# The end of a down projection: one row pair more left over, another tile order, and sums in an order written out by hand

## The chip, the cores and the metric

The kernel runs on one core of a Trainium2 chip. Its metric is the device time of one execution in microseconds (us). The engines are named as the profile names them: PE is TensorE (matrix products), DVE is VectorE, ACT is ScalarE, POOL is GpSimd, SP is SyncE, which here only issues transfers (DMAs).

## The reference

One decoder layer on 512 tokens of width 1024, in float32: a conditioned mixer (mLSTM heads beside a convolution group), then a causal ConvFFN. The change touches only the last product of the ConvFFN and the normalised, gated addition that follows it:

```python
u = rms_norm(x, ffn_pre_g[l]) * (1.0 + sc2) + sh2
up = causal_dwconv(u @ ffn_up[l], ffn_conv_w[l], ffn_conv_b[l])
a, gt = jnp.split(up, 2, axis=-1)
f = (jax.nn.silu(gt) * a) @ ffn_down[l]          # 512 x 2816 by 2816 x 1024
x = x + g2 * rms_norm(f, ffn_post_g[l])
```

`rms_norm` needs the sum of squares over a token's whole row of 1024 before any of its outputs can be scaled.

## The kernel before

**The down projection in seven products.** `f` is 512 tokens by 1024 columns and is computed as a two by two block product with seven products in place of eight. The contraction over 2816 rows runs in `NM` = 11 row pairs (`m`, two blocks of 128 rows each). Each of the products p1 to p7 has two accumulators in PSUM, one for each `q` (128 tokens of a half of 256). Every float32 operand is split in two parts, `h` and `l`, and `mm3` makes one product of 128x128 by 128x512 out of three matmuls.

A first phase runs p1, p5, p6 and p7 over all pairs and leaves sums of them in SBUF: `sp1`, `su`, `s3`, `sp5`. A second phase runs p2, p3 and p4 (`prod2`). The output has four tiles of 128 tokens, `tt` 0 to 3, each in two halves (`hf`) of 512 columns; `q = tt % 2`. Tiles 0 and 1 are p2 + sp1 and p3 + su. Tiles 2 and 3 are p4 + s3 in their first half; their second half is `sp5`, complete since the first phase, squared and already multiplied by the gain row (L1104).

**The second phase's loop (L1106 to L1122).** For each pair `m` the operands are made: `forms_g2(m)` (the activation side, L1034) and `forms2(m)` (the weight side, L1025: one subtraction, then `parts` splits `b2`, `b4` and `t4` into `h` on ACT and `l` on VectorE). Then SP issues transfers: for four of the values of `m` a pair of loads of the residual rows (`xrs`, L1110 to L1114, tied to `M2`), then `load2(m + 3)` (three loads of weight parts, L1019) and `load_g2(m + 5)`. For `m < M2` all eighteen matmuls of the pair follow: p2, p3 and p4, each for both `q`. The pairs from `M2` on are left for the end.

**The end (L1123 to L1142).** For each tile in turn the left pairs' matmuls are run, and then, for each half that is not complete, a sum (PSUM plus SBUF, L1134), a sum of squares on ACT (`sq_sum`, L608: an ACTIVATE and a read of its accumulator) and a scaling by the gain row (L1137). `token_factor` (L612) then makes the tile's factor: a 128x1 step on VectorE (L615) and a power on POOL (L617). Two output steps follow (L1141), each with a store, the first half's from SP's queue and the second half's from ACT's.

**What sets the order.** The instructions of PE and SP stay in the order of the program. VectorE, ACT and POOL are ordered by a planner at build time, which takes, of what its own model of time holds ready, the instruction that stands earliest in the program. `in_order()` is a block in which those three engines too keep the order that is written, by ordering edges that are no instructions; until now it is used elsewhere, not in the second phase. Weight parts rotate through 20 buffers (`wpool`), six for each pair; raw weights through two `raws` and the two halves of `more`.

Of the kernel before, what the change touches and what calls it, by code (L numbers as in the profile page):

```python
# [14 lines left out]
ALU = mybir.AluOpType  # L15
# [4 lines left out]
T = 512  # L20
KT = D // P
NT = T // P
# [30 lines left out]
def decoder_layer(ctx, tc, w_glu0, x, c, adaT, vecs, w_glu, w_qko, w_v0, w_v, w_out, w_up, w_down, out):  # L53
    nc = tc.nc
    V, S, G, PE = nc.vector, nc.scalar, nc.gpsimd, nc.tensor
# [13 lines left out]
    @contextmanager  # L69
    def in_order():  # L70

        traced = nc.cur_bb.bb.instructions
        first = traced[-1]
        yield
        a = next(i for i in reversed(range(len(traced))) if traced[i] is first) + 1
        last = {}
        for ins in traced[a:]:
            if ins.engine in (V.engine, S.engine, G.engine):
                if ins.engine in last:
                    tc.add_manual_dep(ins, last[ins.engine].name, mybir.DependencyInfo(mybir.DependencyClass.NoSync, mybir.DependencyReason.DATA),  # L80
                                      reason="program order")
                last[ins.engine] = ins

    def slot(name, dt=F32):
        return slots.tile([P, T], dt, tag="t", name=name)
# [100 lines left out]
    def mm3(ps, a, b, start, stop):  # L186

        PE.matmul(ps, a[0], b[0], start=start, stop=False)  # L188
        PE.matmul(ps, a[0], b[1], start=False, stop=False)  # L189
        PE.matmul(ps, a[1], b[0], start=False, stop=stop)  # L190
# [28 lines left out]
    first = []  # L219
# [25 lines left out]
    for tt in range(NT):  # L245
# [11 lines left out]
        if tt == NT - 1:  # L257
# [9 lines left out]
                    op0=ALU.add)  # L267
    g32 = const.tile([P, KT], F32, name="g32")
    V.tensor_scalar(out=g32, in0=vcols("mix_pre_g", 0, KT), scalar1=RD, scalar2=None, op0=ALU.mult)
    xr = [slot(f"xr{j}") for j in range(KT)]  # L270
# [32 lines left out]
    for k in range(KT):  # L303
        wk = []
        r = adas.tile([P, D], F32, tag="ada", name=f"wglu0_{k}")
# [285 lines left out]
    def row(i, make, name, queue=nc.scalar):  # L591

        rows = make(name) if make is not cvtile else [make(f"{name}r{hf}") for hf in range(2)]
        for hf, r in enumerate(rows):
            queue.dma_start(r, rows_d[i][hf * T : (hf + 1) * T].partition_broadcast(P))
        return rows
# [8 lines left out]
    def cvtile(name):  # L605
        return cvs.tile([P, T], F32, tag="cvs", name=name)

    def sq_sum(src, col, name):  # L608
        junk = small.tile([P, T], BF16, tag="junk", bufs=1, name=f"{name}junk")
        S.activation(junk, src, AF.Square, accum_out=col)  # L610

    def token_factor(sq, name):  # L612

        t = small.tile([P, 1], F32, tag="tt", name=f"{name}t")
        V.tensor_scalar(out=t, in0=sq[:, :1], scalar1=sq[:, 1:2], scalar2=D * EPS, op0=ALU.add, op1=ALU.add)  # L615
        r = small.tile([P, 1], F32, tag="tr", name=f"{name}r")
        G.tensor_tensor(out=r, in0=t, in1=mhalf[:, :1], op=ALU.pow)  # L617
        return r

    def tok(tt):  # L620
        return slice(tt * P, (tt + 1) * P)
# [171 lines left out]
    def chain_sums(tt):  # L793

        ps = banks[tt]
        sq_sum(ps, msq[:, 2 * tt + 1 : 2 * tt + 2], f"mixb{tt}")
        un = adas.tile([P, D], F32, tag="ada", name=f"un{tt}")
        uns[tt] = [un[:, :T], un[:, T:]]
        V.tensor_tensor(out=uns[tt][1], in0=ps, in1=g1r[1], op=ALU.mult)
        return token_factor(msq[:, 2 * tt : 2 * tt + 2], f"rm{tt}")  # L800

    def chain_x(tt, r):

        xsq = small.tile([P, 2], F32, tag="xsq", name=f"xsq{tt}")
        for hf, m in enumerate((mg[tt], uns[tt][1])):
            V.scalar_tensor_tensor(out=x1[tt][hf], in0=m, scalar=r, in1=x1[tt][hf], op0=ALU.mult, op1=ALU.add)
            sq_sum(x1[tt][hf], xsq[:, hf : hf + 1], f"x1_{tt}_{hf}")
        for hf, un in enumerate(uns[tt]):
            V.tensor_tensor(out=un, in0=x1[tt][hf], in1=gs2r[hf], op=ALU.mult)
        return token_factor(xsq, f"rf{tt}")  # L810
# [53 lines left out]
    with in_order():  # L864
# [3 lines left out]
        r = chain_sums(0)  # L868
        up_split(1, raw1, slots, "t")
        r = chain_x(0, r)  # L870
# [3 lines left out]
        r = chain_sums(1)  # L874
        up_split(1, raw1, slots, "t")
        r = chain_x(1, r)
# [4 lines left out]
        r = chain_sums(2)  # L881
        turn_out(1)
        r = chain_x(2, r)
# [4 lines left out]
        r = chain_sums(3)  # L888
        up_split(2, raw2, wpool, "w")
        r = chain_x(3, r)  # L890
# [29 lines left out]
    NM = NF // 2  # L920
# [26 lines left out]
    for i in range(NF):  # L947
        if i < NE:
            pa, pg = early[i]
        else:  # L950
# [4 lines left out]
            if i == 19:  # L955
# [4 lines left out]
                g2r = row(3, lambda n: [wide[:, :T], wide[:, T:]], "g2")  # L960
# [15 lines left out]


    M1 = NM - 2
    M2 = NM - 2
    fsq = const.tile([P, 2 * NT], F32, name="fsq")  # L980
    p1 = [atbank(f"p1_{q}") for q in range(2)]
    p5 = [cvbank(f"p5_{q}") for q in range(2)]
# [42 lines left out]
    def forms2(m):  # L1025

        r = loaded.pop(m)
        V.tensor_tensor(out=quarter(r, 2), in0=quarter(r, 0), in1=quarter(r, 2), op=ALU.subtract)
        return parts(r, [(f"b2_{m}", 0), (f"b4_{m}", 1), (f"t4_{m}", 2)])

    def load_g2(m):
        nc.sync.dma_start(kept[:, m % 5, :], g2_d[m])
# [8 lines left out]
    def part(form, q):  # L1041
        return tuple(z[:, q * P : (q + 1) * P] for z in form)
# [53 lines left out]
    def prod2(m, which, q):  # L1096
        a12, a22, s4 = g2[m]
        ps, form, w = {"p2": (p2, a12, "b2"), "p3": (p3, s4, "b4"), "p4": (p4, a22, "t4")}[which]
        mm3(ps[q], part(form, q), w2[m][w], m == 0, m == NM - 1)
# [5 lines left out]
    xrs = []  # L1105
    for m in range(NM):  # L1106
        if m >= G2A:
            g2[m] = forms_g2(m)
        w2[m] = forms2(m)
        if M2 - NT <= m < M2:  # L1110
            tt = m - M2 + NT
            xrs.append([cvtile(f"xr{tt}_{hf}") if tt < 2 else slot(f"xr{tt}_{hf}") for hf in range(2)])
# [4 lines left out]
        if m + 5 < NM:  # L1117
            load_g2(m + 5)
        if m < M2:
            for which in ("p2", "p3", "p4"):  # L1120
                for q in range(2):
                    prod2(m, which, q)  # L1122
    for tt in range(NT):  # L1123
        q = tt % 2
        for which in ("p2", "p3") if tt < 2 else ("p4",):
            for m in range(M2, NM):
                prod2(m, which, q)
        res, xr = [], xrs[tt]
        for hf, pair in enumerate(((p2[q], sp1[q]), (p3[q], su[q])) if tt < 2 else ((p4[q], s3[q]), None)):
            if pair is None:  # L1130
                res.append(sp5[q])
                continue
            ps, z = pair
            V.tensor_tensor(out=z, in0=ps, in1=z, op=ALU.add)  # L1134
            sq_sum(z, fsq[:, 2 * tt + hf : 2 * tt + hf + 1], f"dn{tt}_{hf}")
            m = slot(f"fo{tt}_{hf}")
            V.tensor_tensor(out=m, in0=z, in1=g2r[hf], op=ALU.mult)  # L1137
            res.append(m)
        r = token_factor(fsq[:, 2 * tt : 2 * tt + 2], f"ro{tt}")
        for hf in range(2):  # L1140
            V.scalar_tensor_tensor(out=res[hf], in0=res[hf], scalar=r, in1=xr[hf], op0=ALU.mult, op1=ALU.add)  # L1141
            (nc.scalar if hf else nc.sync).dma_start(out[tok(tt), hf * T : (hf + 1) * T], res[hf])  # L1142


def _layout(i):
# [65 lines left out]
```

## Time and profile before

| what | value |
|---|---|
| median of 3 runs | 783.6 us (783.5 to 783.65) |
| profiled execution, its own time | 782.93 us |
| its span, first to last instruction | 781.2 us |
| mean granted TensorE clock | 0.996 |
| VectorE busy over the span | 590.7 us in 938 instructions |
| ACT busy | 407.6 us |
| POOL busy | 384.8 us |
| DMA moved | 124.28 MB, mean 159 GB/s |

In timelines a row has the start (us from the span's start), the duration, the engine, the line in the kernel, the operation, the tile written and the tiles read (buffer numbers left out, so `p` is any of p1 to p7 and `t_10l` is the `l` part of a weight form of pair 10), shapes, and in brackets the idle time before it with what ended it. Durations overlap at their ends: the next instruction of an engine starts before the one ahead of it has fully drained, so prices are read from start to start.

### The profile page before, as it was taken

Reading aid. Unit: us, or ns where it says so; the run is one execution under the profiler, and the core shown is the slowest. Engines: PE = TensorE matmul, PEld = TensorE weight load, DVE = VectorE, ACT = ScalarE, POOL = GpSimd, SP = SyncE. Lnnn points to the kernel's source line nnn. Section 1 sums busy time; section 2 is a strip of 40 time slices with the busy share of each in tenths; the row PEclk is TensorE's granted clock in tenths of the full one; section 3 lists DMA queues with packets and bytes.
Section 4 is the critical chain, followed back from the end, with each engine's and each line's share of the span. In section 5 each row is a group of like instructions: output and inputs, shape, how many; then the busy total and the mean of one; then the engine's idle time right before and its main releaser. Section 6 shows DMA issues by size and latency. Waiting matters only on the chain.

```text
span 781.2 us, 10573 instructions
## 1 busy us (share of the span) xinstructions
PE 762.0 (98%) x3683; PEld 635.5 (81%) x3683; DVE 590.7 (76%) x938; ACT 407.6 (52%) x766; POOL 384.8 (49%) x313
## 2 busy tenths in 40 slices
PE   7899999999999999999999999999999999999995
PEld 4688898878888888888888998888888888888883
DVE  6659999999999433555868798666555678698986
ACT  6576428668655554482244545444444444456752
POOL 3689758779779434333661456444445440000001
PEclk9999999999999999999999999999999999999998
DMA  8983213303117432424962653332233321778852
GB/s 291 327 300 122 105 60 108 135 29 109 55 60 248 152 110 79 147 108 151 380 220 83 259 205 136 128 128 98 99 121 122 128 99 51 285 258 263 296 205 107
DMA packets 35977, 124.28 MB, mean 159 GB/s; under 512 B 4146, under 2 KB 5586, under 8 KB 29908
## 3 DMA queue, kind: packets, MB, share of 16 engines
q1 hardware_dynamic: 24084, 95.15, 34.5%
q10 hardware_dynamic: 11840, 28.46, 10.2%
q8 instruction: 29, 0.48, 0.2%
q14 instruction: 24, 0.20, 0.1%
HBM read 112.17 MB, written 11.42 MB: 158 GB/s over the span
## 4 chain that ended last, share of the span: by engine, by line
PE 80%; DVE 14%; DMA 2%; ACT 1%; POOL 1%; issue 1%; SPq 0%; DVEq 0%; POOLq 0%; ACTq 0%
PE up L189 10%; PE up L188 10%; PE up L190 10%; DVE cv L661 6%; PE p L190 4%; PE p L188 4%; PE p L189 4%; PE glu L189 3%; PE glu L190 3%; PE glu L188 3%; PE qko L188 3%; PE qko L189 3%; PE qko L190 3%; PE mixa L190 2%; PE mixa L188 2%; PE mixa L189 2%
## 5 line engine op out<-in xcount | busy, mean ns | idle before, releaser
L661 DVE SCALAR_TENSOR_TENSOR cv<-gt,cvw,cv 128x506 f32<-128x506 f32 (+24 forms) x200 | 134.3, 730 | 0.4
L617 POOL TENSOR_TENSOR ro0r<-ro0t,mhalf 128x1 f32<-128x1 f32 x1 | 0.9, 925 | 125.8 <-DVE ro0t L615 125.8
L171 POOL TENSOR_TENSOR wup_1024l<-wup,wup_1024h 128x512 fp32r<-128x512 f32 x20 | 27.3, 1367 | 31.7 <-ACT wup_1024h L170 27.9
L171 POOL TENSOR_TENSOR wup_0l<-wup,wup_0h 128x512 fp32r<-128x512 f32 x20 | 27.7, 1387 | 29.8 <-ACT wup_0h L170 29.8
L657 POOL TENSOR_TENSOR cs<-cs,cs 128x510 f32<-128x510 f32 (+3 forms) x32 | 41.8, 1308 | 0.2
L171 POOL TENSOR_TENSOR wup_1536l<-wup,wup_1536h 128x512 fp32r<-128x512 f32 x20 | 28.2, 1409 | 27.4 <-ACT wup_1536h L170 27.4
L189 PE MATMUL up<-u2l,wup_0h 128*128 128x512 f32 (+1 forms) x100 | 36.5, 365 | 0.2 <-DVE u2l L830 0.2
L188 PE MATMUL up<-u2h,wup_0h 128*128 128x512 f32 (+1 forms) x100 | 36.5, 365 | 0.0
L188 PE MATMUL up<-u2h,wup_1024h 128*128 128x512 f32 (+1 forms) x100 | 36.4, 364 | 0.0
L190 PE MATMUL up<-u2h,wup_0l 128*128 128x512 f32 (+1 forms) x100 | 36.4, 364 | 0.0
L188 PE MATMUL up<-u2h,wup_512h 128*128 128x512 f32 (+1 forms) x100 | 36.4, 364 | 0.0
L189 PE MATMUL up<-u2l,wup_512h 128*128 128x512 f32 (+1 forms) x100 | 36.4, 364 | 0.0
L188 PE MATMUL up<-u2h,wup_1536h 128*128 128x512 f32 (+1 forms) x100 | 36.4, 364 | 0.0
L189 PE MATMUL up<-u2l,wup_1536h 128*128 128x512 f32 (+1 forms) x100 | 36.4, 364 | 0.0
L190 PE MATMUL up<-u2h,wup_512l 128*128 128x512 f32 (+1 forms) x100 | 36.4, 364 | 0.0
L190 PE MATMUL up<-u2h,wup_1536l 128*128 128x512 f32 (+1 forms) x100 | 36.4, 364 | 0.0
L190 PE MATMUL up<-u2h,wup_1024l 128*128 128x512 f32 (+1 forms) x100 | 36.4, 364 | 0.0
L189 PE MATMUL up<-u2l,wup_1024h 128*128 128x512 f32 (+1 forms) x100 | 36.3, 363 | 0.0
L155 DVE SCALAR_TENSOR_TENSOR junk<-ada,cb 128x1024 bf16<-128x1024 f32 x20 | 30.8, 1542 | 5.6 <-DMA ada<-in_adaT 5.3
L171 POOL TENSOR_TENSOR wup_512l<-wup,wup_512h 128x512 fp32r<-128x512 f32 x20 | 27.2, 1360 | 14.6 <-ACT wup_512h L170 14.6
L655 ACT ACTIVATE cs<-gt,cvw 128x511 f32<-128x511 f32 (+4 forms) x40 | 27.2, 713 | 5.0 <-POOL cs L657 4.1
L171 POOL TENSOR_TENSOR wqko_1024l<-wqko,wqko_1024h 128x512 fp32r<-128x512 f32 x12 | 16.6, 1382 | 21.8 <-PE v L189 12.3
(1061 smaller groups left out, 2682.1 us busy)
## 6 DMA issues: line engine op xcount, KB each, us to landing
wup<-in_w_up SPq DMA_DIRECT2D x22, 1024.0 KB, 7.3
wqko<-in_w_qko SPq DMA_DIRECT2D x12, 1024.0 KB, 4.9
ada<-in_adaT ACTq DMA_DIRECT2D x20, 512.0 KB, 5.5
ada<-in_adaT SPq DMA_DIRECT2D x16, 512.0 KB, 5.8
wo<-in_w_out SPq DMA_DIRECT2D x8, 1024.0 KB, 9.3
spare<-in_adaT ACTq DMA_DIRECT2D x12, 512.0 KB, 7.5
wglu<-in_w_glu SPq DMA_DIRECT2D x5, 1024.0 KB, 7.7
wd<-in_w_down SPq DMA_DIRECT2D x6, 768.0 KB
```

The source lines that it names most:

```text
L155: t = V.scalar_tensor_tensor(out=junk, in0=r, scalar=1.0, in1=cb, op0=ALU.mult, op1=ALU.mult, accum_out=mod[:, i : i + 1])
L171: (eng or G).tensor_tensor(out=lo[:, :n], in0=src, in1=hi[:, :n].bitcast(F32), op=ALU.subtract)
L188: PE.matmul(ps, a[0], b[0], start=start, stop=False)
L189: PE.matmul(ps, a[0], b[1], start=False, stop=False)
L190: PE.matmul(ps, a[1], b[0], start=False, stop=stop)
L617: G.tensor_tensor(out=r, in0=t, in1=mhalf[:, :1], op=ALU.pow)
L655: S.activation(t[:, d:], cvx[j][:, : T - d], AF.Copy, scale=w(CK - 1 - d))
L657: G.tensor_tensor(out=side[:, d:], in0=side[:, d:], in1=t[:, d:], op=ALU.add)
L661: last_tap = V.scalar_tensor_tensor(out=cp[:, d:], in0=cvx[j][:, : T - d], scalar=w(CK - 1 - d), in1=cp[:, d:], op0=ALU.mult, op1=ALU.add)
```

## The change

`M2` goes from `NM - 2` to `NM - 3`: pair 8 is no longer run in the loop, and three pairs are left for the end. The residual loads, tied to `M2`, move from `m` = 5 to 8 to `m` = 4 to 7. The end takes tiles 2 and 3 first, then 0 and 1. Sums, squares, scalings, factors, output steps and stores are cut into small functions and written in one fixed order, inside `in_order()`. Of tiles 2 and 3 the second half is stored first. No arithmetic is added or taken away.

```diff
-    M2 = NM - 2
+    M2 = NM - 3
...
-    for tt in range(NT):
-        q = tt % 2
+    def last_products(tt):
         for which in ("p2", "p3") if tt < 2 else ("p4",):
             for m in range(M2, NM):
-                prod2(m, which, q)
-        res, xr = [], xrs[tt]
+                prod2(m, which, tt % 2)
+
+    def last_sums(tt, only=None):
+
+        q, res = tt % 2, []
         for hf, pair in enumerate(((p2[q], sp1[q]), (p3[q], su[q])) if tt < 2 else ((p4[q], s3[q]), None)):
+            if only not in (None, hf):
+                continue
             if pair is None:
                 res.append(sp5[q])
                 continue
             ps, z = pair
             V.tensor_tensor(out=z, in0=ps, in1=z, op=ALU.add)
             sq_sum(z, fsq[:, 2 * tt + hf : 2 * tt + hf + 1], f"dn{tt}_{hf}")
+            res.append(z)
+        return res
+
+    def last_scale(tt, res, first=0):
+        for n in range(1 if tt >= 2 else len(res)):
+            hf = n + first
             m = slot(f"fo{tt}_{hf}")
-            V.tensor_tensor(out=m, in0=z, in1=g2r[hf], op=ALU.mult)
-            res.append(m)
-        r = token_factor(fsq[:, 2 * tt : 2 * tt + 2], f"ro{tt}")
-        for hf in range(2):
-            V.scalar_tensor_tensor(out=res[hf], in0=res[hf], scalar=r, in1=xr[hf], op0=ALU.mult, op1=ALU.add)
-            (nc.scalar if hf else nc.sync).dma_start(out[tok(tt), hf * T : (hf + 1) * T], res[hf])
+            V.tensor_tensor(out=m, in0=res[n], in1=g2r[hf], op=ALU.mult)
+            res[n] = m
+        return res
+
+    def last_factor(tt):
+        return token_factor(fsq[:, 2 * tt : 2 * tt + 2], f"ro{tt}")
+
+    def last_out(tt, res, r, hf):
+        V.scalar_tensor_tensor(out=res[hf], in0=res[hf], scalar=r, in1=xrs[tt][hf], op0=ALU.mult, op1=ALU.add)
+        (nc.scalar if hf else nc.sync).dma_start(out[tok(tt), hf * T : (hf + 1) * T], res[hf])
+
+    with in_order():
+        last_products(2)
+        last_products(3)
+        z2 = last_sums(2)
+        last_scale(2, z2)
+        r2 = last_factor(2)
+        z3 = last_sums(3)
+        last_out(2, z2, r2, 1)
+        last_out(2, z2, r2, 0)
+        last_products(0)
+        last_scale(3, z3)
+        r3 = last_factor(3)
+        z0 = last_sums(0, 0)
+        last_out(3, z3, r3, 1)
+        last_out(3, z3, r3, 0)
+        z0 += last_sums(0, 1)
+        last_scale(0, z0)
+        last_products(1)
+        z1 = last_sums(1, 0)
+        r0 = last_factor(0)
+        last_scale(1, z1)
+        z1 += last_sums(1, 1)
+        z1 = [z1[0], *last_scale(1, z1[1:], 1)]
+        last_out(0, z0, r0, 0)
+        r1 = last_factor(1)
+        last_out(0, z0, r0, 1)
+        last_out(1, z1, r1, 0)
+        last_out(1, z1, r1, 1)
```

## The prediction

> **What bounds the kernel now.** I read the page first, then the chain of waits from 762 us on, then each engine's timeline from 740 us to the end. TensorE (PE) is busy for 98% of the span:
>
> ```profile
> PE 762.0 (98%) x3683; PEld 635.5 (81%) x3683; DVE 590.7 (76%) x938; ACT 407.6 (52%) x766; POOL 384.8 (49%) x313
> ```
>
> But the end is not TensorE's. In the chain of waits (start, us, what) the last PE piece is at 764.46; from there to the last instruction everything is VectorE (DVE):
>
> ```profile
> 764.46 0.24 PE p L190
> ...
> 777.49 0.66 DVE sp L1141
> ```
>
> PE's timeline (start, us, line) and VectorE's say why. The eighteen products of row pair 8 begin at 759.08, pairs 9 and 10 follow, and the last matmul starts at 771.10:
>
> ```profile
> 759.08 0.39 PE L188 MATMUL p<-b_8h,g2h 128*128 128x512 f32 x1
> ...
> 764.29 0.39 PE L190 MATMUL p<-b_10h,g2l 128*128 128x512 f32 x1
> ...
> 771.10 0.39 PE L190 MATMUL p<-t_10h,g2l 128*128 128x512 f32 x1
> ```
>
> ```profile
> 759.35 0.69 DVE L927 TENSOR_TENSOR t_10l<-wd,t_10h 128x512 fp32r<-128x512 f32 x1
> 764.72 0.69 DVE L1134 TENSOR_TENSOR sp<-p,sp 128x512 f32<-128x512 f32 x1 [4.69 <-PE p L190]
> 765.45 0.69 DVE L1137 TENSOR_TENSOR fo<-sp,g2r 128x512 f32<-128x512 f32 x1
> 766.08 0.69 DVE L1134 TENSOR_TENSOR su<-p,su 128x512 f32<-128x512 f32 x1
> ...
> 768.05 0.20 DVE L615 TENSOR_SCALAR ro0t<-fsq 128x1 f32<-128x1 f32 x1
> 768.17 0.69 DVE L1137 TENSOR_TENSOR fo<-sp,g2r 128x512 f32<-128x512 f32 x1
> ...
> 769.41 1.41 DVE L1141 SCALAR_TENSOR_TENSOR fo<-fo,ro0r,xr 128x512 f32<-128x512 f32 x2
> 770.73 0.68 DVE L1137 TENSOR_TENSOR fo<-su,g2r 128x512 f32<-128x512 f32 x1
> 771.33 0.68 DVE L1134 TENSOR_TENSOR s<-p,s 128x512 f32<-128x512 f32 x1
> ...
> 777.41 0.74 DVE L1141 SCALAR_TENSOR_TENSOR sp<-sp,ro3r,xr 128x512 f32<-128x512 f32 x1
> ```
>
> VectorE stands idle for 4.69 us, until the first tile is summed up, and then has 24 instructions to run, without a gap, from 764.72 to 778.15: it ends more than 6 us after TensorE. What can be gained is that idle time, and what limits the gain is how late the last tile's product comes. The same rows give the prices from start to start: 0.73 for a scaling right behind the sum that it reads (764.72 to 765.45), 0.63 for a large one ahead of a sum (765.45 to 766.08), 0.60 between others (770.73 to 771.33), 0.66 for each output step (1.32 for the two from 769.41), 0.12 for the 128x1 step (768.05 to 768.17), and 0.43 from the start of a group's last matmul to the sum that reads it (764.29 to 764.72).
>
> **The change: TensorE.** Three pairs times eighteen matmuls are left either way, 54 of them from 759.08, and the last starts at 771.10, so 0.227 us each. The new order only regroups them: nine for tile 2 (p4, pairs 8 to 10), nine for tile 3, then p2 and p3 of tile 0, then p2 and p3 of tile 1, 2.04 us a group. The sums that read these six groups can start at 761.32, 763.37, 765.41, 767.45, 769.49 and 771.53. I cost the regrouping at nothing, on one condition: tile 2's group needs t_10l at the eighth of its matmuls, at 759.08 + 7 x 0.227 = 760.67, where before pair 10's t4 was first needed by the 46th of the 54, at 759.08 + 45 x 0.227 = 769.3. VectorE has finished it at 759.35 + 0.69 = 760.04. The cover is 0.63 us; what comes later than that is paid one to one.
>
> **The factor chain.** Each tile needs sum, square (ACT), 128x1 step, power (POOL), output step. After the first sum ACT shows
>
> ```profile
> 765.51 0.63 ACT L610 ACTIVATE dn_0junk<-sp 128x512 bf16<-128x512 f32 x1 [7.18 <-DVE sp L1134]
> 766.04 0.19 ACT L610 ACTIVATION_READ_ACCUMULATOR dn_0junk<-sp 128x1 f32 x1
> ```
>
> so 0.79 from the sum to the square and 0.72 to the end of its accumulator read. In the tail VectorE is always late, so what it waits when it is early is not seen there. The mixer's end has the same helper with VectorE waiting:
>
> ```profile
> 410.52 0.19 ACT L610 ACTIVATION_READ_ACCUMULATOR x_1junk<-x 128x1 f32 x1
> 410.74 0.21 DVE L615 TENSOR_SCALAR rf0t<-xsq 128x1 f32<-128x1 f32 x1 [0.42 <-ACT x_1junk L610]
> ...
> 411.62 1.42 DVE L814 SCALAR_TENSOR_TENSOR un<-un,rf0r,sh2r 128x512 f32<-128x512 f32 x2 [0.67 <-POOL rf0r L617]
> ...
> 413.55 0.21 DVE L615 TENSOR_SCALAR rm1t<-msq 128x1 f32<-128x1 f32 x1
> ...
> 414.78 0.75 DVE L806 SCALAR_TENSOR_TENSOR x<-mg,rm1r,x 128x512 f32<-128x512 f32 x1 [0.43 <-POOL rm1r L617]
> ```
>
> That is 0.03 from the read to the 128x1 step, and from there to the output step 0.88 or 1.23. The two prices come from the power:
>
> ```profile
> 768.33 0.93 POOL L617 TENSOR_TENSOR ro0r<-ro0t,mhalf 128x1 f32<-128x1 f32 x1 [125.80 <-DVE ro0t L615]
> 772.22 0.54 POOL L617 TENSOR_TENSOR ro1r<-ro1t,mhalf 128x1 f32<-128x1 f32 x1 [2.96 <-DVE ro1t L615]
> ```
>
> 0.93 began beside the scaling at 768.17 (two operands in SBUF), 0.54 beside a sum (one operand in PSUM). So I take 0.88 where a sum follows the 128x1 step (tiles 2 and 3) and 1.23 where a scaling or an output step does (tiles 0 and 1).
>
> The Trainium skill, SBUF — State Buffer, section "Who interferes with whom", has a rule for this: a VectorE instruction with two SBUF inputs and a GpSimd one that reads SBUF lock each other out, and who starts second waits for the whole of the first. The two POOL rows agree for GpSimd as the one that waits. By the rule it could also go the other way, an output step held up by a power already running; where the new order starts a power, the two-input step before it is already under way or the next one waits for that very power, so the sum would be the same.
>
> **The sum, VectorE in its new order.** Sum of tile 2 at 761.32; its scaling 762.05; 128x1 step 761.32 + 0.79 + 0.72 + 0.03 = 762.86; factor ready 763.74. Sum of tile 3 at 763.37 (waits for TensorE 0.39); tile 2's two outputs 764.00 and 764.66; tile 3's scaling 765.32; 128x1 step 765.92; first sum of tile 0 at 766.04; tile 3's factor ready 766.80 (a wait of 0.13), outputs 766.80 and 767.46; second sum of tile 0 at 768.12; scalings 768.75 and 769.35; first sum of tile 1 at 769.95; 128x1 step of tile 0 at 770.56; scaling of tile 1 at 770.68; free at 771.28, but the second sum of tile 1 waits for TensorE until 771.53; its scaling 772.26; first output of tile 0 at 772.86; 128x1 step of tile 1 at 773.52; second output of tile 0 at 773.64; tile 1's factor ready 774.75 (a wait of 0.45); last outputs 774.75 and 775.41.
>
> The last output step started at 777.41: 2.00 us less. Up to tile 1's last sum there is 0.25 us of slack; behind it the path is fixed by TensorE's end. Bounds: with 0.88 for tile 1's factor the last step is at 775.06, a gain of 2.35; with 1.23 for tiles 2 and 3 as well the sum at 771.53 moves to 771.72, and the gain is 1.81.
>
> **Around it.** Behind the last step come an issue and its landing:
>
> ```profile
> DMA to landing us min/median/max: 2.1/2.1/2.1
> ```
>
> The last four outputs still alternate between SP and ACT, 0.66 us or more apart, so this end moves along whole. On ACT the output of tile 2 waits in front of tile 0's first square: it can go at about 764.8, the square is due at 766.8, no loss. The written-out order moves no work off VectorE and adds none; ordering edges on the same engine are no instruction.
>
> Last, the x1 row loads (xr) are tied to M2 and go one row pair earlier on SP's queue: one pair of them, 512 KB, gets ahead of the weight reloads of pairs 7 to 10. The loads, and the reload that is already late, pair 9's, for which VectorE waited:
>
> ```profile
> xr<-x1d SPq DMA_DIRECT2D x8, 256.0 KB, 4.5
> ```
>
> ```profile
> 751.44 0.69 DVE L1028 TENSOR_TENSOR wd<-wd 128x512 f32<-128x512 f32 x1 [0.69 <-DMA wd<-t2d]
> ```
>
> The stretches (last two columns: DMA share, GB/s) show what room there is:
>
> ```profile
> 747.50:750.00 2.50, 2.50 (x12) 2.06 (x11) 2.50 (x5) 1.83 (x4) 0.00 (x0) 1.00 0.60 173
> 750.00:754.50 4.50, 4.50 (x21) 3.74 (x20) 3.81 (x8) 2.79 (x6) 0.00 (x0) 1.00 1.03 392
> 733.00:734.00 1.00, 1.00 (x6) 0.83 (x5) 1.00 (x3) 1.00 (x3) 0.00 (x0) 1.00 0.48 125
> ```
>
> At 392 GB/s the 512 KB take 1.34 us; the two stretches that were not full, 2.5 us at a share of 0.60 and 1 us at 0.48, hold 1.00 + 0.52 = 1.52 us, so pair 9's reload should land as before. The reloads of pairs 8 to 10 have one xr pair directly ahead of them as they had, with another number; only pair 7's has a new one.
>
> Sum: the profiled execution took 782.93 us (span 781.2), so 780.93; the median of the runs is 783.6, 0.67 above it, so 781.6.
>
> **Rivals.** First, a stall of TensorE in place of VectorE's: the gaps don't take up the 512 KB, and pair 9's reload lands 1.34 us later. Everything from 751.44 to 760.04 on VectorE is one unbroken row of work in its timeline, so t_10l ends at 761.38, 0.71 past its cover; the gain shrinks to 1.29 and the time is 782.3. For it: the 0.69 wait. Against: the gaps. Chance 0.14.
>
> Second, the hand-written order waits more than I list: VectorE runs strictly in order, and each output step now stands right behind the factor it needs. If two more of these waits cost a full long factor chain less the short one (0.35 each), and one more sum slips behind its neighbour by 0.6, the gain is 0.7 and the time 782.9. Against it is the 0.25 us of slack ahead of tile 1's last sum. Chance 0.10.
>
> Third, slower: t4 of pair 10 is now needed 8.9 us earlier (first use at 769.3 before, at the seventh matmul, 760.44, now). If work that the planner is free to place ahead of the fixed block, or a late reload, puts t_10l back, TensorE stops with all four tiles behind it. It decides from 0.63 + 2.00 = 2.6 us of delay; with 4.5 us the time is 785.5. Nothing in the trace is that late; the planner's order before the block should not change, as those instructions stand earlier in the program. Chance 0.07.
>
> Fourth, the change doesn't do what it says: the end is set by the outputs' queues and not by VectorE, and the time stays 783.6. The 2.1 us landings, equal for all, speak against it. Chance 0.05.
>
> **How the numbers follow.** Forecast 0.64, with 781.1 to 781.9 as its own range (the bounds 2.35 and 1.81, and 0.1 for the runs' spread). To hold 8 in 10 the range takes in the first rival and most of the second: 781.1 to 782.8. About 0.2% (1.6 us) is what a measurement tells from no change; faster by more means below 782.0: the forecast's 0.64, and 0.06 of the first rivals with smaller delays, 0.70. Within 0.2%: 0.22. Slower: 0.08.
>
> **What would show it.** In the changed profile TensorE should run without a gap to a last matmul start near 771.1, VectorE's first sum should start near 761.3, tile 1's last sum within 0.3 of 771.5, and the last output step near 775.4. A gap on TensorE between 760 and 762 would prove the first or third rival; a sum of tile 1 starting more than 0.3 behind TensorE's last group, the second.

## The result: 1.7 us less, and the profile after

The median of the changed kernel is 781.88 us, against 783.56 for the kernel before in the same rounds: a ratio of 0.9977, with a 95% interval of 0.9969 to 0.9986. By the ratio that is 1.8 us, between 1.1 and 2.4: small, but clear of no change. The forecast was 781.6, 2.00 less. The profiled execution of the changed kernel took 782.39 us (span 780.6), though, only 0.54 less than the one of before, so the two profiles have to be taken apart before the 1.7 can be seen in them.

The page: TensorE is as busy as it was (761.7 us, 762.0 before).

TensorE's timeline (start, us, line). The left-over matmuls start at 760.51, the one that needs `t_10l` first at 762.09, the last at 772.52:

```profile
760.51 0.39 PE L188 MATMUL p<-t_8h,g2h 128*128 128x512 f32 x1
...
762.09 0.39 PE L189 MATMUL p<-t_10l,g2h 128*128 128x512 f32 x1
...
772.52 0.39 PE L190 MATMUL p<-b_10h,s 128*128 128x512 f32 x1
```

VectorE's timeline, whose two last output steps share the last row (the second starts 0.67 behind the first, 1.41 less the 0.74 that one takes, so at 776.92):

```profile
759.88 0.68 DVE L927 TENSOR_TENSOR t_10l<-wd,t_10h 128x512 fp32r<-128x512 f32 x1
762.75 0.69 DVE L1138 TENSOR_TENSOR s<-p,s 128x512 f32<-128x512 f32 x1 [2.19 <-PE p L190]
...
764.29 0.21 DVE L615 TENSOR_SCALAR ro2t<-fsq 128x1 f32<-128x1 f32 x1
764.79 0.69 DVE L1138 TENSOR_TENSOR s<-p,s 128x512 f32<-128x512 f32 x1 [0.28 <-PE p L190]
...
767.32 0.21 DVE L615 TENSOR_SCALAR ro3t<-fsq 128x1 f32<-128x1 f32 x1
...
768.18 0.75 DVE L1155 SCALAR_TENSOR_TENSOR sp<-sp,ro3r,xr 128x512 f32<-128x512 f32 x1
...
772.95 0.69 DVE L1138 TENSOR_TENSOR su<-p,su 128x512 f32<-128x512 f32 x1 [0.22 <-PE p L190]
...
774.94 0.21 DVE L615 TENSOR_SCALAR ro1t<-fsq 128x1 f32<-128x1 f32 x1
...
776.25 1.41 DVE L1155 SCALAR_TENSOR_TENSOR fo<-fo,ro1r,xr 128x512 f32<-128x512 f32 x2 [0.44 <-POOL ro1r L617]
```

The chain of waits (start, us, what) at its end:

```profile
764.52 0.24 PE p L190
...
772.20 0.92 POOL ro0r L617
773.12 2.08 issue
775.20 1.03 POOLq L1248
776.25 0.75 DVE fo L1155
```

Read alone, this chain misleads: it goes back over POOL, and calls 2.08 us of it "issue". POOL's own row for the last power, `ro1r` (further down), says what it waited for, `[2.11 <-DVE ro1t L615]`, tile 1's 128x1 step, and that hangs on the square, on the sum at 772.95, and so on TensorE.

VectorE now starts its sums 2.24 us behind the first matmul of pair 8, where it was 5.64 (759.08 to 764.72), and it is no longer behind TensorE when the last product comes: it waits 0.22 us for it. I call **the tail** the time from the start of TensorE's last matmul to the start of the last output step. It was 777.41 - 771.10 = 6.31 us; it is 776.92 - 772.52 = 4.40 us. That is 1.91 us less, and it is where the gain is.

The other 1.4 us that the pair of profiles seems to have lost lie ahead of the change. TensorE's matmuls with the weight form `t_0h`, by whose first start I date the down projection (times of first and last start), before and after:

```profile
L188 PE MATMUL p<-t_0h,fh x6: 389/389/389, 667.9 to 671.3; 128*128 128x512 f32 x6
```

```profile
L188 PE MATMUL p<-t_0h,fh x6: 389/389/389, 669.3 to 672.7; 128*128 128x512 f32 x6
```

The projection begins 1.4 us later in this one execution, in code that did not change, and from there to the last matmul it is 103.2 us in both. One place of that is seen, a wait of TensorE near the mixer's end which the profile of before lacks:

```profile
400.71 0.27 PE L585 MATMUL gT<-ident,gains 128*16 128x128 f32 x1 [1.25 <-DVE gains L783]
```

But the start moves without it too. Over the fourteen profiles of this study it lies between 667.9 and 669.5. So each kernel below is read by three numbers: the start of the projection, the time from there to the last matmul (103.1 to 103.4 when TensorE doesn't stall), and the tail. What follows the last output step is the same everywhere, 5.43 to 5.52 us to the execution's own time.

| kernel | start | to last matmul | tail | own time of the profile | median | ratio to before (95%) |
|---|---|---|---|---|---|---|
| before | 667.9 | 103.2 | 6.31 | 782.93 | 783.56 | |
| changed | 669.3 | 103.2 | 4.40 | 782.39 | 781.88 | 0.9977 (0.9969 to 0.9986) |
| again | 669.5 | 103.1 | 4.39 | 782.44 | 781.98 | 0.9977 (0.9968 to 0.9985) |
| pairs_only | 668.8 | 103.2 | 5.63 | 783.08 | 783.14 | 0.9986 (0.9970 to 1.0002) |
| order_only | 669.1 | 103.4 | 7.26 | 785.19 | 784.41 | 1.0007 (0.9998 to 1.0016) |
| planner_free | 668.4 | 103.2 | 4.52 | 781.59 | 781.63 | 0.9975 (0.9965 to 0.9985) |
| factor_early | 668.5 | 103.1 | 4.09 | 781.18 | 781.22 | 0.9966 (0.9949 to 0.9983) |
| loads_old_place | 668.2 | 104.3 | 4.40 | 782.33 | 781.89 | 0.9978 (0.9963 to 0.9992) |
| four_pairs | 668.3 | 105.0 | 4.39 | 783.17 | 784.67 | 1.0009 (0.9995 to 1.0023) |
| four_forms_first | 668.5 | 103.3 | 4.39 | 781.65 | 781.48 | 0.9988 (0.9968 to 1.0007) |
| four_reordered | 668.3 | 103.1 | 3.51 | 780.35 | 780.72 | 0.9960 (0.9944 to 0.9977) |
| four_again | 669.2 | 103.1 | 3.52 | 781.28 | 781.24 | 0.9977 (0.9966 to 0.9988) |
| four_loads_last | 668.4 | 108.6 | 3.51 | 785.90 | 784.98 | 1.0017 (0.9995 to 1.0040) |
| three_loads_last | 668.8 | 104.8 | 4.09 | 783.22 | 782.94 | 0.9989 (0.9975 to 1.0004) |

The median of the kernel before was 783.87, 783.66 and 783.45 in the three groups of experiments. The tails repeat to 0.01 us (4.40 and 4.39, 3.51 and 3.52); the medians of one kernel differ by 0.1 and 0.5. So a mechanism in the tail is judged by the tail, and whether it pays by the medians.

### The profile page after: what moved, and what is told of

It reads as the page before. It is cut to its first block, busy times and chain, and to the rows that moved or that the text cites. A ratio compares the mean times of both kernels' runs of the same rounds, so it can differ in the third digit from the quotient of the medians.

```text
span 780.6 us, 10572 instructions
## 1 busy us (share of the span) xinstructions
PE 761.7 (98%) x3683; PEld 635.0 (81%) x3683; DVE 591.3 (76%) x938; ACT 407.6 (52%) x766; POOL 383.9 (49%) x313
## 4 chain that ended last, share of the span: by engine, by line
PE 80%; DVE 10%; DMA 4%; issue 3%; POOL 1%; ACT 1%; ACTq 0%; POOLq 0%; DVEq 0%; SPq 0%
PE up L189 10%; PE up L188 10%; PE up L190 10%; DVE cv L661 5%; PE qko L188 4%; PE qko L189 4%; PE qko L190 4%; PE p L190 4%; PE p L189 4%; PE p L188 4%; PE glu L189 3%; PE glu L190 3%; PE glu L188 3%; DMA spare<-in_adaT 2%; PE o L466 2%
```

## Experiments: which part brings it

The theory: the gain is idle time of VectorE that is used, and it needs both parts. A third left-over pair lets the sums start earlier; the new order leaves only one tile behind TensorE's end. The rival: one of the two does it all.

**The changed kernel again**, as the measure for the others.

> The changed kernel once more, beside the three variants. Call the tail the time from the start of TensorE's last matmul to the start of VectorE's last output step: 6.31 us before, 4.39 in the changed kernel's profile, 4.31 by the prediction's sum. Theory (VectorE starts 3.4 us earlier, the end is then fixed by TensorE's last product): the tail is 4.3 to 4.5 again, the time 1.8 to 2.0 us under before, whatever the first 700 us do in one execution. Rival (the gain comes from something ahead of the tail, such as earlier transfers): the tail moves with the execution and the gap on TensorE does not stay at 399 us.

Tail 4.39, median 781.98. Its projection starts at 669.5 without the wait at 400.

**The pairs alone.** The kernel before with `M2 = NM - 3`; the residual loads, tied to `M2`, move along.

```diff
-    M2 = NM - 2
+    M2 = NM - 3
```

> The kernel before with M2 = NM - 3 alone: three pairs left, tiles 0 to 3 as before, the planner's order. Theory: VectorE's first sum starts 3.4 us earlier as in the changed kernel, but the planner puts tile 3's sum, scaling and 128x1 step behind the outputs of tiles 1 and 2; by the prediction's prices the last sum starts 1.1 us after TensorE allows it, tile 3's factor is then waited for alone (0.8), and the tail is 5.6: 0.7 us under before, 782.9. Rival (the third pair is all that counts): tail 4.4, 781.7. Rival (the order is all that counts): tail 6.3, 783.6.

Measured 5.63. Its rows on TensorE and VectorE:

```profile
771.98 0.39 PE L190 MATMUL p<-t_10h,g2l 128*128 128x512 f32 x1
```

```profile
762.21 0.69 DVE L1134 TENSOR_TENSOR sp<-p,sp 128x512 f32<-128x512 f32 x1 [2.18 <-PE p L190]
...
773.55 0.68 DVE L1134 TENSOR_TENSOR s<-p,s 128x512 f32<-128x512 f32 x1
...
776.94 0.75 DVE L1141 SCALAR_TENSOR_TENSOR fo<-fo,ro3r,xr 128x512 f32<-128x512 f32 x1 [0.66 <-POOL ro3r L617]
```

The sums start as early as in the changed kernel (2.18 us idle in place of 4.69), but the old order has tile 2 still open when TensorE ends: the last sum runs at 773.55, where its product allows it at 771.98 + 0.43 = 772.41. That is 0.68 us off the tail, a third of the gain.

**The order alone.** The changed kernel with `M2 = NM - 2`, so with the residual loads in their old place too.

```diff
-    M2 = NM - 3
+    M2 = NM - 2
```

> The changed kernel with M2 = NM - 2: the new tile order and the written-out order, but two pairs left. Theory: VectorE's first sum can start no earlier than before (six matmuls from 763.16, so 764.72), and by the prediction's prices its 24 instructions then run behind TensorE all the way, with two more waits for factors: tile 1's last sum starts 2.9 us after TensorE allows it and the tail is 7.2, so 0.9 us slower than before, 784.5. Rival (the order is what brings the gain): tail 4.4, 781.7.

Measured 7.26, longer than before. VectorE's rows:

```profile
766.13 0.69 DVE L1138 TENSOR_TENSOR s<-p,s 128x512 f32<-128x512 f32 x1 [4.13 <-PE p L190]
...
775.79 0.68 DVE L1138 TENSOR_TENSOR su<-p,su 128x512 f32<-128x512 f32 x1
...
779.09 1.41 DVE L1155 SCALAR_TENSOR_TENSOR fo<-fo,ro1r,xr 128x512 f32<-128x512 f32 x2 [0.44 <-POOL ro1r L617]
```

With two pairs the first sum comes 6.37 us ahead of TensorE's last matmul (772.50) in place of 9.77, and VectorE, which has the same list to run, reaches tile 1's last sum 2.86 us after the product allows it. It starts them as far ahead as before (771.10 - 764.72 = 6.38) and needs 13.63 us from there to the last output step, where it was 12.69. The instructions are the same 24; what is added are waits that the old order doesn't have: 0.5 us ahead of tile 1's outputs (the 0.44 for `ro1r`), and three shorter ones for the squares and factors of tiles 2 and 3, 0.14 to 0.2 each. So the parts are not additive: -0.68 alone, +0.95 alone, -1.91 together.

**The order left to the planner.** The changed kernel without the block `in_order()` at the end.

```diff
-    with in_order():
+    if True:
         last_products(2)
...
```

> The changed kernel without the in_order block: three pairs left and the new tile order, but VectorE, ACT and POOL ordered by the planner. Theory: its order differs only in the middle of tiles 0 and 1 and in tile 1's 128x1 step, which comes after tile 0's second output, so nothing covers the factor's wait: tail 4.5 to 4.7, 0.2 us over the changed kernel. Rival (writing out the order is a main part): tail 5.3 or more, 1 us over it.

Measured 4.52: the written-out order itself is worth 0.12 us, and the medians (781.63 and 781.98) don't show it. What counts is the order of the tiles and the third pair.

## Experiments: what ends the tail now

**Tile 1's factor asked for earlier.** In the changed kernel the 0.44 us wait for `ro1r` is the only wait in the tail besides TensorE's.

```diff
-        last_out(0, z0, r0, 0)
         r1 = last_factor(1)
+        last_out(0, z0, r0, 0)
         last_out(0, z0, r0, 1)
```

> The changed kernel with tile 1's factor asked for ahead of tile 0's first output step in place of behind it. Measured from the start of TensorE's last matmul to the start of the last output step (4.40 us in the changed kernel). Theory (the end is the chain sum, square, factor, outputs of tile 1, in which 0.44 us is a wait for GpSimd's power, made long by the two-SBUF output step beside it): the one-column addition starts as soon as the square ends, the power lies beside tile 0's outputs, the wait goes: 4.05 to 4.15, some 0.3 under the changed kernel. Rival (the power is stretched by the two output steps, and the wait only moves): 4.4 or more. The end of the span itself can differ by what comes ahead of the last matmul, up to 1.5 us from one execution to another.

Measured 4.09, and the wait is gone. VectorE's and POOL's rows:

```profile
773.59 0.21 DVE L615 TENSOR_SCALAR ro1t<-fsq 128x1 f32<-128x1 f32 x1
773.72 1.41 DVE L1155 SCALAR_TENSOR_TENSOR fo<-fo,ro0r,xr 128x512 f32<-128x512 f32 x2
775.04 1.41 DVE L1155 SCALAR_TENSOR_TENSOR fo<-fo,ro1r,xr 128x512 f32<-128x512 f32 x2
```

```profile
773.88 0.98 POOL L617 TENSOR_TENSOR ro1r<-ro1t,mhalf 128x1 f32<-128x1 f32 x1 [1.65 <-DVE ro1t L615]
```

The power is as long as before (0.98) but lies beside tile 0's two output steps, and these are not lengthened by it (1.41 for two, as everywhere). So of a VectorE and a GpSimd instruction that overlap here, it is GpSimd's that gets longer. By the rule that the prediction cites (the Trainium skill, SBUF — State Buffer, "Who interferes with whom") it could also have been an output step that waits; no row here shows that. The median, 781.22, is 0.7 below the changed kernel's in its two rounds; 0.3 of that is in the tail.

**A fourth pair.** `M2 = NM - 4`, pair 10's forms in buffers of another pool, the same written order. The residual loads move one more pair earlier with `M2`, here and in the next three kernels.

```diff
-    M2 = NM - 3
+    M2 = NM - 4
...
+        return parts(r, names) if m < NM - 1 else parts(r, names, lambda name: slot(name, F32R))
```

> Four row pairs left for the end in place of three, in the same written order; the last pair's weight forms stand in buffers of another pool. Theory (with three pairs the end is already fixed by TensorE's last product, no more by the start of the sums): the tail stays at 4.3 to 4.5, and no gain over the changed kernel; a loss of 0 to 1.2 us if the last weight form is ready later than TensorE asks for it, which is now 13.8 us ahead of its last matmul. Rival (each pair left over takes as much off as the third did, because the end still waits for VectorE's list of sums): a further 1.3 us or more off the tail.

The tail is 4.39: unchanged, as the theory has it, since it hangs on TensorE's last product and no longer on the start of the sums. But TensorE stalls, for the third form of pair 9:

```profile
758.67 0.50 PE L189 MATMUL p<-t_9l,g2h 128*128 128x512 f32 x1 [1.58 <-DVE t_9l L927]
```

From the start of the projection to the last matmul it is 105.0 in place of 103.2, more than the wait itself, and more than the 0 to 1.2 I expected. The median of the runs is another 1.5 above this profile. The granted clocks of the runs go with it: 783.0 to 784.2 us at 0.998, 784.6 to 787.4 us at 0.996 and 0.995. A spell of half clock like the one shown further down (3.5 us at 0.52) would lower the mean by 0.002, by my estimate: 3.5 x 0.48 / 781. No profile shows such a run, so this stays an estimate.

**Four pairs, third forms first.** The same, with `t4` of the left-over pairs made ahead of their `b2` and `b4`, which are only needed by tiles 0 and 1.

```diff
+        w = parts(r, names[2:], *make)
+        late.append(lambda: w.update(parts(r, names[:2], *make)))
+        return w
...
+    for rest in late:
+        rest()
```

> Four row pairs left over, the third forms of the left-over pairs made first, but the written order of the changed kernel. It separates the two halves of the version that did best. Theory (with four pairs TensorE stalled 1.6 us because a third weight form came late, and that is all it lost; the tail itself is fixed by the written order): no stall of TensorE, tail 4.3 to 4.5, time as the changed kernel, 781.5 to 782.3. Rival (forms first don't mend the stall; what mended it is something in the tail's order): a stall of 1 us or more and a time above the kernel before.

No stall, 103.3; tail 4.39; median 781.48. So the late third form was all that four pairs lost (the median is now close to the profile's 781.65), and with it mended they are worth nothing by themselves:

```profile
756.41 0.69 DVE L927 TENSOR_TENSOR t_10l<-wd,t_10h 128x512 fp32r<-128x512 f32 x1
...
772.24 0.69 DVE L1148 TENSOR_TENSOR su<-p,su 128x512 f32<-128x512 f32 x1 [1.27 <-PE p L190]
```

`t_10l` starts 15.4 us ahead of the last matmul (771.82), 12.6 in the changed kernel, and in front of tile 1's last sum VectorE has 1.27 us to spare. This spare time is what another order can use.

**Four pairs, reordered.** Tile 0's factor ahead of tile 1's first sum, tile 0's outputs ahead of tile 1's last sum, tile 1's factor right behind its last scaling.

```diff
+        r0 = last_factor(0)
         z1 = last_sums(1, 0)
-        r0 = last_factor(0)
+        last_out(0, z0, r0, 0)
+        last_out(0, z0, r0, 1)
         last_scale(1, z1)
         z1 += last_sums(1, 1)
         z1 = [z1[0], *last_scale(1, z1[1:], 1)]
-        last_out(0, z0, r0, 0)
         r1 = last_factor(1)
-        last_out(0, z0, r0, 1)
```

> Four row pairs left, the third forms of the left-over pairs made first, and the order altered so that VectorE has only tile 1's last sum, square, factor and outputs to do behind TensorE's last matmul: tile 0's factor ahead of tile 1's first sum, tile 0's outputs ahead of tile 1's last sum, tile 1's factor right behind its last scaling. Theory (the floor is that chain alone: 0.79 + 0.72 + 0.03 + 0.88 + one output step of 0.6 to 0.7): tail 3.0 to 3.6, about 0.9 us under the changed kernel, if TensorE doesn't stall for a weight form. Rival (DVE's list as a whole sets the end, and the four pairs only move work ahead that is paid for by a late weight form): tail 3.6 to 4.4 or a later last matmul, time as the changed kernel or above.

Tail 3.51. TensorE's and VectorE's rows:

```profile
771.41 0.39 PE L190 MATMUL p<-b_10h,s 128*128 128x512 f32 x1
```

```profile
771.84 0.69 DVE L1148 TENSOR_TENSOR su<-p,su 128x512 f32<-128x512 f32 x1
772.56 0.69 DVE L1157 TENSOR_TENSOR fo<-su,g2r 128x512 f32<-128x512 f32 x1
773.38 0.21 DVE L615 TENSOR_SCALAR ro1t<-fsq 128x1 f32<-128x1 f32 x1
774.25 1.42 DVE L1165 SCALAR_TENSOR_TENSOR fo<-fo,ro1r,xr 128x512 f32<-128x512 f32 x2 [0.66 <-POOL ro1r L617]
```

Nothing but tile 1's own chain is left behind TensorE's end: 0.43 to the sum, 1.54 to the 128x1 step, 0.87 to the first output, 0.67 to the second. Its power is a short one, as no two-operand instruction runs beside it. The median is 780.72.

**The same once more**, on another chip.

> The version with four pairs, third forms first and the altered order once more, on another chip, as the measure for the next kernel. Theory (the profile's tail of 3.51 holds in each execution, what differs is what comes ahead of it): tail 3.5, median 780.4 to 781.2. Rival (it was a lucky profile): tail 3.8 or more, median at 781.6 or above.

Tail 3.52, median 781.24, just above what I expected; the projection started at 669.2 in its profile. The version beats the kernel before in both rounds (0.9960 and 0.9977). That it beats the changed kernel as a whole is shown by its tail, 0.9 us shorter, and not by the ratios, whose intervals overlap.

## Experiments: the loads that moved along

The change also moved the loads of the outputs' second addend (`xr`, 2 MB) one row pair earlier on SP's queue. I had called that free.

**The loads in their old place.**

```diff
-        if M2 - NT <= m < M2:
-            tt = m - M2 + NT
+        if M2 + 1 - NT <= m < M2 + 1:
+            tt = m - M2 - 1 + NT
```

> The changed kernel with the 512 KB of loads for the outputs' second addend at the row pairs where the kernel before has them, one pair later. Theory (these transfers find free time on the queues and nobody waits for them): the tail from the last matmul to the last output step stays at 4.4 and the time within 0.1% of the changed kernel. Rival (their new place delays the weights of the last pairs, which is where the predicted 0.08 us more went): TensorE's last matmul is earlier and the time lower by 0.5 us or more.

The theory's figures hold, its reason doesn't: the tail is 4.40 and the median the changed kernel's, but somebody does wait. In the profile VectorE waits 2.04 us for pair 9's reload, and TensorE 0.79 us for `t_10l`. VectorE's subtractions (L1028) of pairs 8 and 9, and TensorE's rows around its wait:

```profile
747.85 0.68 DVE L1028 TENSOR_TENSOR wdmore<-wdmore 128x512 f32<-128x512 f32 x1
...
753.32 0.69 DVE L1028 TENSOR_TENSOR wd<-wd 128x512 f32<-128x512 f32 x1 [2.04 <-DMA wd<-t2d]
```

```profile
760.77 0.40 PE L188 MATMUL p<-t_10h,g2h 128*128 128x512 f32 x1
761.96 0.51 PE L189 MATMUL p<-t_10l,g2h 128*128 128x512 f32 x1 [0.79 <-DVE t_10l L927]
762.30 0.39 PE L190 MATMUL p<-t_10h,g2l 128*128 128x512 f32 x1
```

The same two subtractions in the changed kernel, without a wait:

```profile
747.70 0.68 DVE L1028 TENSOR_TENSOR wdmore<-wdmore 128x512 f32<-128x512 f32 x1
...
752.59 0.68 DVE L1028 TENSOR_TENSOR wd<-wd 128x512 f32<-128x512 f32 x1
```

On the queue pair 9's reload has two `xr` loads directly ahead of it and two directly behind it in both kernels. What the loads' place does change is VectorE's order in this stretch, which the planner makes. With the loads in the old place it is the order of the kernel before: five instructions between the two subtractions, and a wait. In the changed kernel there are eight. There `t_5l`, which frees the buffer, also comes earlier, so that pair 9's reload is issued 76.1 us behind the projection's start in place of 77.4. In the old place two more loads follow at 750.43, behind pair 10's reload and before pair 9's has been seen to land; whether they slow it, these profiles don't separate from the order. The medians don't show the loss, so I can't say that each execution has it.

**The loads last**, behind the last reload and in the order in which the tiles are finished, once with four pairs and once with three (and the early factor). I expected a reload to gain from it. The wait of 1.05 us that I meant, in `four_reordered`, is ahead of the last subtraction, so it was for pair 10's reload and not for pair 9's.

```diff
-        if M2 - NT <= m < M2:
-            tt = m - M2 + NT
...
+        if m >= NM - NT:
+            tt = (m - NM + NT + 2) % NT
...
```

> The same with the loads for the outputs' second addend put behind the last weight reload, in the order in which the tiles are finished. Theory (what spreads its executions is the reload of pair 9, for which VectorE waited 1.05 us in the profile, and which shares the queue with these 2 MB): that wait goes, TensorE has no stall, tail 3.5, a median at or up to 0.5 us below the version before and fewer executions above 782. Rival (the loads now come too late for tile 2's outputs, or other forms get ahead of pair 10's third form): VectorE waits for a load or TensorE for t_10l, and the time is 0.5 us or more above.

> The changed kernel (three pairs) with tile 1's factor asked for early and these loads behind the last weight reload. Theory (with three pairs nothing waits for the reloads, so the loads' place is worth nothing): tail 4.1, time 781.0 to 781.5 as with the early factor alone. Rival (the loads' place matters for the last reloads here too): VectorE's forms end earlier or later by 1 us or more, and the time differs by 0.5 us.

Both went the rivals' way. With all eight loads behind the last reload, pair 10's, VectorE waits for that reload, and the third form of pair 10 comes late. Three pairs:

```profile
755.91 0.69 DVE L1028 TENSOR_TENSOR wd<-wd 128x512 f32<-128x512 f32 x1 [2.35 <-DMA wd<-t2d]
```

```profile
763.08 0.50 PE L189 MATMUL p<-t_10l,g2h 128*128 128x512 f32 x1 [0.85 <-DVE t_10l L927]
```

That is 104.8 to the last matmul and a median of 782.94, 1.7 above the same kernel with the loads early (`factor_early`, 781.22). In that one the subtraction doesn't wait:

```profile
755.75 0.69 DVE L1028 TENSOR_TENSOR wd<-wd 128x512 f32<-128x512 f32 x1
...
759.36 0.69 DVE L927 TENSOR_TENSOR t_10l<-wd,t_10h 128x512 fp32r<-128x512 f32 x1
```

Two things changed together here. The first is the transfer. Of the reload's three parts the profiles give the landing of the first two (the first part is the least and the second the most of each line, in us from issue), with three pairs and the loads early, then last, and with four pairs early (`four_reordered`), then last:

```profile
DMA to landing us min/median/max: 4.9/5.0/5.1
DMA to landing us min/median/max: 4.1/5.1/6.1
DMA to landing us min/median/max: 3.8/3.9/4.1
DMA to landing us min/median/max: 3.9/5.3/6.6
```

The second part, with the loads close behind it, lands 1.0 and 2.5 us later. The other thing is the planner's order. Counted from the projection's start, pair 10's subtraction comes at the same time in both kernels with three pairs (87.1 and 87.3). With the loads early VectorE has done other forms by then, and `t_10l` follows 3.61 us later; with the loads last it has stood still for 2.35 us, does these forms afterwards, and `t_10l` follows 6.43 us later, at 762.34. How much of the 1.7 us belongs to the transfer and how much to the order is not shown.

Four pairs, TensorE and then the stretches (us, busy of PE, PEld, DVE, ACT, POOL, granted clock, DMA share, GB/s):

```profile
761.34 0.51 PE L189 MATMUL p<-t_10l,g2h 128*128 128x512 f32 x1 [2.35 <-DVE t_10l L927]
```

```profile
761.30:762.10 0.80, 0.76 (x3) 0.66 (x4) 0.80 (x2) 0.00 (x0) 0.00 (x0) 1.00 0.00 0
762.10:765.60 3.50, 3.50 (x10) 2.67 (x10) 3.46 (x6) 0.61 (x2) 0.00 (x0) 0.52 0.02 5
```

TensorE stalls 0.79 us (for the activation form `g2l`) and, two matmuls on, 2.35 us, and 0.8 us after it has started again its clock is granted at half for 3.5 us: ten matmuls in a stretch in which fifteen start at 0.227 each. So 3.1 us of waits cost 5.4 us (108.6 against 103.2). The Trainium skill, TensorE: Matmul & The Clock Gate, section "What's actually happening", tells of a gate that passes half or all of the clock by how busy the array has lately been, with a window of about 3.4 us; these rows agree, in the two levels and in the length.

## Why the prediction was right, step by step

- **What bounds it, and TensorE.** Right. The 54 matmuls take 12.01 us from the first to the last start (12.02 before): the regrouping cost nothing, and there was no gap. The last matmul stands at 772.52 and not near 771.1 only because the projection began 1.4 us later.
- **VectorE's start.** 761.32 was 2.24 behind the first left-over matmul; measured 762.75 - 760.51 = 2.24.
- **The factor chain.** 1.54 from sum to 128x1 step was forecast (0.79 + 0.72 + 0.03); measured 764.29 - 762.75 = 1.54. The two prices fell where they were put: 767.32 to 768.18 is 0.86 (0.88 forecast) for tile 3, where a sum follows. For tile 1, 774.94 to 776.25 is 1.31, and 1.23 was forecast. The powers show why:

```profile
767.61 0.54 POOL L617 TENSOR_TENSOR ro3r<-ro3t,mhalf 128x1 f32<-128x1 f32 x1 [2.48 <-DVE ro3t L615]
772.20 0.92 POOL L617 TENSOR_TENSOR ro0r<-ro0t,mhalf 128x1 f32<-128x1 f32 x1 [4.05 <-DVE ro0t L615]
775.23 0.98 POOL L617 TENSOR_TENSOR ro1r<-ro1t,mhalf 128x1 f32<-128x1 f32 x1 [2.11 <-DVE ro1t L615]
```

  Beside an output step (0.74) the power takes 0.98, beside a scaling (0.69) 0.92, beside a sum 0.54. This is the term that was mis-sized, and it is nearly all of the miss: 1.91 in the tail in place of 2.00. The prediction gave an output step the price of a scaling; the profile of before already has a power beside output steps, `ro2r` at 773.54, and it takes 0.98.
- **The waits.** 0.25 us of slack ahead of tile 1's last sum, measured 0.22; 0.45 for tile 1's factor, measured 0.44; 0.39 for tile 3's sum, measured 0.28.
- **Around it.** From the last output step to the end 5.47 us, 5.52 before: the queues of the outputs move along whole, and the fourth rival is out.
- **The loads called free.** The sign was missed. The 0.69 us wait at L1028 is gone in the changed kernel, and `t_10l` is ready 762.09 - 760.56 = 1.53 us ahead of its use, where 0.63 was forecast. The prediction looked at what the loads get ahead of, and not at the two that no longer stand behind pair 10's reload. And it held, against the third rival, that the planner's order ahead of the block should not change: it did change with the loads' place. The first rival (a stall of TensorE for `t_10l`) is a real one: it is what happens in the profile with the loads in the old place, 0.79 us. What kept it away was this side effect, which the prediction did not reckon with, and not the gaps. That part was luck.
- **"Paid one to one."** That was said of a late `t_10l`. Waits of 0.79 and 1.58 us cost 1.1 and 1.8 us to the last matmul, and 3.1 us cost 5.4, with the clock halved in between. So the third rival would have turned the sign at some 0.3 us less than the 2.6 us of delay that I gave.
- **The second rival** (the written order waits more) did not come: its waits are the three listed above, and the written order is 0.12 us shorter than the planner's.

What stays open: why the projection starts up to 1.5 us earlier or later from one execution to another; why the runs of `four_pairs` lie 1.5 us above its profile, where the granted clocks speak for a spell of half clock, but no profile shows one; and how much of what the loads' place does is the transfers and how much the planner's order.

## What to carry to other kernels

An end that hangs on one engine's list has two handles that only work together: when the list can start, and what of it must come after the last product; cost both against the same timeline before turning either. Measure such an end from the last product to the last output step, since that repeats to 0.01 us where whole executions differ by 1 or 2. And a transfer that nobody waits for is not free: in these kernels it was better ahead of the last reload that somebody does wait for than behind it. After moving it, read the order of the other engines again, since a planner may make another one.

## What the runs showed of the hardware that I had not expected

- A transfer landed later where others were issued behind it on the same queue: the second 256 KB part of pair 10's reload took 6.1 and 6.6 us with eight loads of 256 KB behind the reload, 5.1 and 4.1 with none.
- A stall of TensorE cost about 0.3 us more than the wait in its row (1.1 and 1.8 us for 0.79 and 1.58). The rows of the first show why: the wait is counted from the end of the matmul ahead, 0.40 behind its start, where the next would have started 0.23 behind it; and the start after the stalled one comes 0.34 later (761.96 to 762.30).
- After waits of 0.79 and 2.35 us, with two matmuls between them, the clock was granted at half for 3.5 us; after a single wait of 1.58 us it stayed at 1.00.
